# A hybrid streaming layer on one core: right-hand sums on VectorE alone, and output rows of two token blocks formed during the next block

## The chip, the core and the metric

The kernel runs on one core of one Trainium2 chip. The metric is the device time of one execution in microseconds, lower being better. Before the change it is 2352.13 us (median of 3 runs, 2347.12 to 2352.42). The engines are called as in the profile: PE (TensorE, the products), PEld (its weight loads), DVE (VectorE), ACT (ScalarE), POOL (GpSimd) and SP (SyncE, which issues the DMAs).

## What is computed

One layer of a streaming encoder over 2048 prompt tokens and 32 sample tokens of width 1024, all in float32: a norm, one input projection, attention and a state-space scan side by side, an output projection with a residual, and then a SwiGLU feed-forward network with a residual. The change lies in the last part alone:

```python
    h2 = _rmsnorm(x, lw['ln2_g']) * (1.0 + sc2) + sh2
    ff = (jax.nn.silu(h2 @ lw['w_gate']) * (h2 @ lw['w_up'])) @ lw['w_down']
    x = x + g2 * ff
```

`w_gate` and `w_up` are 1024 x 2816, `w_down` is 2816 x 1024.

## The kernel before

**Blocks and layers.** The feed-forward part begins at about 950 us of the span and runs to its end. It works on three token blocks one after the other (`PIECES`, `sb` = 0, 1, 2), of 704, 704 and 672 tokens. In each block there are four layers: `L.i` = 0 is gate and up (11 units `u`, each with a gate and an up half `m` = 0, 1), and `L.i` = 1, 2, 3 are thirds of the down projection (2 units each), whose results gather in the SBUF tiles `acc`. Features lie on the partitions, tokens in the free dimension, half a block (352 or 336 tokens) to a product.

**Seven products.** Each unit multiplies a left 2 x 2 arrangement (weights) with a right one (activations, the tiles `q00`, `q01`, `q10`, `q11`, in code `b11`, `b12`, `b21`, `b22`) by a scheme with seven products (`PRODUCTS`, steps p = 0 to 6) in place of eight. That needs sums of weight quarters on the left (`wr`, formed on POOL) and four sums of quarters on the right, once per layer, formed in `prepare_right` six steps ahead: t1 = b12 - b11, t3 = b22 - b12, t2 = b22 - t1 and t4 = b21 - t2, each written over one of its inputs (t1 and t2 over b11).

**Split operands.** A float32 product is made of three, of a high part and a rest on each side (`mm3`): ACT rounds the high part (`bh` for the right, `wh` for the left), DVE subtracts to get the rest (`bl`, `wl`). One step is thus 2 halves `m` x 4 x 3 = 24 products on PE, with results in the PSUM banks `fx`, `fy`, `fz`. After each step `finish` takes banks up: `c` tiles on ACT, DVE and POOL for gate and up, `acc` on DVE for down.

**Output rows.** When a unit `u` of the last down layer has done steps 5 and 6, `out_rows` begins for its half of the 1024 features: it loads residual rows `xr` through SP (6 buffers), then for each of 2 or 4 pieces of up to 128 tokens transposes four `acc` slices on PE into a PSUM bank (`fo`; the two banks of tag `ft` are shared with the transposes that build the next block's activations), adds the bank to `xr` on DVE, and stores the row through SP. A block has 12 such pieces. The generators stand in the list `live`, and each is moved on by one piece after every step.

**What sets the order.** The code gives a program order; a scheduler then places the instructions of each engine, and may pull an instruction forward as far as its inputs and free buffers allow. Each engine then runs its own list in order.

Of the kernel before, what the change touches and what calls it, by code (L numbers as in the profile page):

```python
# [16 lines left out]
MULT, ADD, SUB = ALU.mult, ALU.add, ALU.subtract  # L17
# [56 lines left out]
def hybrid_kernel(  # L74
# [10 lines left out]
    V, A, P, PE, SP = nc.vector, nc.scalar, nc.gpsimd, nc.tensor, nc.sync  # L85
    dbg = dbg or {}

    def tt(e, out, a, b, op):
        e.tensor_tensor(out, a, b, op=op)  # L89
# [10 lines left out]
    def act(out, a, func=AF.Copy, **kw):  # L100
        A.activation(out, a, func, **kw)  # L101
# [10 lines left out]
    def split(hi, lo, src, eh, el):  # L112
        cp(eh, hi, src)
        tt(el, lo, src, f(hi), SUB)
# [4 lines left out]
    def mm3(out, ah, al, bh, bl, start, stop, more=False):  # L119

        mm(out, ah, bh, start, False, more)
        mm(out, ah, bl, False, stop and al is None, more)
        if al is not None:
            mm(out, al, bh, False, stop, more)
# [83 lines left out]
    def advance(g, n=1):  # L208
        for _ in range(n):
            if next(g, None) is None:  # L210
                return
# [1226 lines left out]
    def h_steps(sb):  # L1438
        q = quads(4)
        qd[sb, 0] = q  # L1440
        w, col = HALF[sb], 0
        for grp in (PIECES[sb][0:3], PIECES[sb][3:6]):
            xs = []
            for j, r0, n in grp:
                m = 128 if j < NPT else DEC
                x = fp_["q"].tile([128, D], F32, tag="xf", name="xf", bufs=3)
                SP.dma_start(x[0:m], x1_d[j * 128:j * 128 + m])
                act(x[0:m], x[0:m], scale=r2[0:m, j:j + 1])
                xs.append((x, m, 0 if j < NPT else 1))
                yield 1  # L1450
            for k in range(KD):
                pb = fp_["t"].tile([128, 384], F32, tag="ft", name="ft")
                for i, (x, m, s) in enumerate(xs):
                    PE.transpose(pb[:, 128 * i:128 * i + m], x[0:m, k * 128:(k + 1) * 128], ident[0:m, 0:m])
                c = col
                o = grp[0][1]
                for s in range(2):
                    left = sum(n for j, _, n in grp if (j >= NPT) == s)
                    while left:
                        h, at = divmod(c, w)  # L1460
                        n = min(left, w - at)
                        act(q[k // 4][h][:, k % 4, at:at + n], pb[:, o:o + n], AF.Identity,
                            scale=sc2[:, k, s:s + 1], bias=sh2[:, k, s:s + 1])
                        c, o, left = c + n, o + n, left - n
                yield 1
            col = c
# [39 lines left out]
    def start_unit(n):  # L1506

        if n < len(steps) and steps[n][0].i == 0:
            L, u, _ = steps[n]
            raw[L, u] = [{t: quarter(L, u, m, t, wtile(4)) for t in ("21", "22", "11", "12")} for m in range(2)]  # L1510
            for r in raw[L, u]:
                r["s1"] = wtile(4)
                tt(P, r["s1"], r["21"], r["22"], ADD)
                tt(P, r["21"], r["11"], r["21"], SUB)
                r["s3"] = r["21"]
# [27 lines left out]
    def bparts(pool, slot, L):  # L1543
        return tuple(pool.tile([128, 4, HW], F32R, tag=f"b{t}{slot}", name=f"b{t}")[:, 0:L.kt, 0:L.w] for t in "hl")
# [55 lines left out]
    def prepare_right(n):  # L1600
        if n >= len(steps) or steps[n][1]:
            return
        L, _, p = steps[n]
        w = L.w
        (b11, b12), (b21, b22) = [[x[:, :, 0:w] for x in row] for row in qd[L.sb, L.i]]

        def parts(i, x):
            bn = PRODUCTS[i][1]
            h, l = bparts(fp_["v"] if i == 0 else pv, bn, L)
            split(h, l, x, A, V)  # L1610
            right[L, i] = (h, l)

        if p == 0:
            parts(0, b11)
            tt(V, b11, b12, b11, SUB)
            tt(P, b12, b22, b12, SUB)
        elif p == 1:
            parts(1, b21)
            parts(3, b11)
            tt(P, b11, b22, b11, SUB)  # L1620
            tt(V, b21, b21, b11, SUB)
        elif p != 3:
            parts(p, {2: b11, 4: b12, 5: b21, 6: b22}[p])
# [79 lines left out]

    def out_rows(L, half, pieces):

        hs_ = slice(half * 512, (half + 1) * 512)
        tiles = [acc[d] for d in range(4 * half, 4 * half + 4)]
        xs = []
        for j, r0, n in [PIECES[L.sb][i] for i in pieces]:
            xr = pwr.tile([128, 512], F32, tag="xr", name="xr", bufs=XR)[0:n]  # L1710
            SP.dma_start(xr, x1_d[j * 128 + r0:j * 128 + r0 + n, hs_])
            xs.append(xr)
        yield 1
        for i, xr in zip(pieces, xs):
            j, r0, n = PIECES[L.sb][i]
            col = sum(x[2] for x in PIECES[L.sb][:i])
            row = j * 128 + r0
            pb = fp_["t"].tile([128, 512], F32, tag="ft", name="fo")[0:n]
            for i in range(4):
                PE.transpose(pb[:, 128 * i:128 * i + 128], tiles[i][:, col:col + n], ident)  # L1720
            tt(V, xr, pb, xr, ADD)
            SP.dma_start((y_sample[0] if j >= NPT else y_prompt[0, row:row + n])[:, hs_], xr)
            yield 1

    live = []
    banks = {}
    cs, gs = {}, {}

    def keep():
        return pv.tile([128, HW], F32, tag="c", name="c", bufs=12)  # L1730
# [31 lines left out]
    def columns(L, j):  # L1762
        ns = L.w - DEC if L.sb == 2 and j else L.w
        return [(0, slice(0, ns))] + ([(1, slice(ns, L.w))] if ns < L.w else [])

    def finish(n):
        L, u, p = steps[n]
        w = L.w
        for m in range(2):
            x, y, z = (banks.get((t, m)) for t in "xyz")  # L1770
            if p in (0, 2, 4):
                c = keep()[:, 0:w]
                if L.i == 0:
                    act(c, x[:, 0:w])
                else:
                    i, j = {0: (0, 0), 2: (0, 1), 4: (1, 1)}[p]
                    d = 4 * u + 2 * m + i
                    for s, cols_ in columns(L, j):
                        act(c[:, cols_], x[:, cols_], scale=g2c[:, d, s:s + 1])
                cs[m, p] = c  # L1780
            if p in (1, 4, 5, 6):
                qd_ = {1: (0, 0), 4: (1, 1), 5: (1, 0), 6: (0, 1)}[p]
                bank = {1: z, 4: y, 5: x, 6: y}[p][:, 0:w]
                c = None if p == 5 else cs.pop((m, {1: 0, 4: 4, 6: 2}[p]))
                (finish_out if L.i else finish_in)(L, u, m, qd_, c, bank)
        if p > 4 and L.i == 3:
            live.append(out_rows(L, u, range(0, 2) if p == 5 else range(2, 6)))

    plain_right("21")
    for m, t in ((0, "21"), (0, "22")):  # L1790
# [26 lines left out]
    for n, (L, u, p) in enumerate(steps):  # L1817
        li = layers.index(L)
        if p == 0:
            start_unit(n + 7)  # L1820
        if L.i == 3 and u == 0 and p == 0 and L.sb < 2:
            coming.append(h_steps(L.sb + 1))
        if L.i == 0 and (u, p) == (5, 0) or L.i in (1, 2) and (u, p) == (0, 1):
            layers[li + 1].load()
        if L.i == 3 and u == 1 and p == 1:
            for _ in chain(*coming):
                pass
        if li == 0 and n > 3:
            advance(sums)
        elif li == 1 and (u, p) == (0, 0):  # L1830
            for _ in sums:
                pass
        load_left(n + FAR)
        prepare(n + AHEAD)
        prepare_right(n + 6)
        bh, bl = right[L, p]
        b = PRODUCTS[p][2]
        first = p in (0, 1, 3)
        for m in range(2):
            ah, al = left[n][m]  # L1840
            if first:
                banks[b, m] = fs1.tile([128, 512], F32, tag=f"{b}{m}", name=f"f{b}")
            dst = banks[b, m][:, 0:L.w]
            for k in range(L.kt):
                mm3(dst, ah[:, k], al[:, k], bh[:, k], bl[:, k], first and k == 0, k == L.kt - 1, not first)
        left.pop(n)
        finish(n)
        for g in chain(coming):
            advance(g, 4)
        for g in list(live):  # L1850
            if next(g, None) is None:
                live.remove(g)
# [53 lines left out]
```

## Time and profile before

| what | value |
|---|---|
| time, median of 3 runs | 2352.13 us (2347.12 to 2352.42) |
| the profiled execution, its own time | 2346.64 us |
| its span, first to last instruction | 2344.8 us |
| mean granted PE clock | 0.969 of full speed |
| DVE row sums `xr` | 36, 24.1 us in all |
| POOL right-hand sums (`q<-q,q`) | 23, 87.5 us in all |

The profile is one execution. A line of the timeline has the start and the length in us, engine, line of code, operation, the tile written and the tiles read, their shape and a count; in square brackets stands how long the engine was idle before it, and what ended that. `x` with a number counts instructions. Line 89 is the helper `tt` (a tensor-tensor operation), 98 is `stt`, 101 is `act`, 117 is `mm`; so groups are told apart by tiles.

### The profile page before, as it was taken

How to read it: one execution, taken by the hardware profiler on the slowest of the kernel's cores; microseconds unless marked ns; L12 is line 12 of the kernel's file. 1: busy time of each engine (PE TensorE's matmuls, PEld its weight loads, DVE VectorE, ACT ScalarE, POOL GpSimd, SP SyncE). 2: the span in 40 equal slices, each digit the busy share in tenths (PEclk: the TensorE clock that was granted, in tenths of full speed). 3: DMA queues.
4: the chain of work that ended last, by engine and by line, in shares of the span. 5: the costliest groups of instructions: out<-in, count | busy, mean ns of one | idle time of the engine just before them, and what ended most of it. 6: DMA issues, size and time to landing. Idle time of an engine off the chain costs nothing. (4 is left out here: it accounts for less than half of the span.)

```text
span 2344.8 us, 39041 instructions
## 1 busy us (share of the span) xinstructions
PE 2215.2 (94%) x13286; PEld 2055.6 (88%) x13286; DVE 1770.5 (76%) x2715; ACT 1258.6 (54%) x2544; POOL 1326.1 (57%) x1195
## 2 busy tenths in 40 slices
PE   7888998897899999999999998999999989999998
PEld 4577776786788888899999997999999989999998
DVE  6878875677877874867668889666588897777887
ACT  6655444456566655544345675444455744445663
POOL 1177775776466664678884246555522466655243
PEclk7899998998899999999999999999999999999999
DMA  7757676675422215567657545443365445433653
GB/s 232 261 168 238 193 218 213 205 237 173 110 73 88 76 53 179 153 200 222 199 178 220 167 137 177 146 138 98 105 200 168 127 146 155 132 107 119 193 162 120
DMA packets 429572, 380.12 MB, mean 162 GB/s; under 512 B 57326, under 2 KB 358986, under 8 KB 429372
## 3 DMA queue, kind: packets, MB, share of 16 engines
q1 hardware_dynamic: 429372, 377.63, 52.7%
q8 instruction: 104, 1.70, 0.3%
q14 instruction: 96, 0.79, 0.1%
HBM read 284.63 MB, written 92.91 MB: 161 GB/s over the span
## 5 line engine op out<-in xcount | busy, mean ns | idle before, releaser
L89 DVE TENSOR_TENSOR wl<-wr,wh 128x512 fp32r<-128x512 f32 (+1 forms) x708 | 717.5, 1031 | 223.1 <-ACT wh L101 218.2
L101 ACT ACTIVATE wh<-wr 128x512 fp32r<-128x512 f32 (+1 forms) x708 | 430.3, 616 | 529.7 <-PE fx L117 290.7
L117 PE MATMUL fx<-bh,wh 128*128 128x352 f32 (+1 forms) x1576 | 508.5, 323 | 9.5 <-DVE acc L98 5.5
L117 PE MATMUL fx<-bl,wh 128*128 128x352 f32 (+1 forms) x1576 | 506.6, 321 | 2.7 <-DVE bl L89 2.7
L117 PE MATMUL fx<-bh,wl 128*128 128x352 f32 (+1 forms) x1576 | 507.3, 322 | 0.0
L89 POOL TENSOR_TENSOR wr<-wr 128x512 f32<-128x512 f32 x256 | 379.8, 1493 | 197.6 <-DVE wl L89 148.0
L117 PEld LDWEIGHTS fx<-bh,wh 128*128 128x128 f32 x1576 | 298.4, 189 | 11.1 <-DVE acc L98 6.1
L117 PEld LDWEIGHTS fx<-bl,wh 128*128 128x128 f32 x1576 | 298.1, 189 | 3.7 <-DVE bl L89 3.7
L117 PEld LDWEIGHTS fx<-bh,wl 128*128 128x128 f32 x1576 | 297.6, 189 | 0.1
L117 PE MATMUL fy<-bh,wl 128*128 128x352 f32 (+1 forms) x792 | 254.0, 321 | 1.4 <-DVE wl L89 1.4
L117 PE MATMUL fy<-bh,wh 128*128 128x352 f32 (+1 forms) x792 | 254.6, 321 | 0.0
L117 PE MATMUL fy<-bl,wh 128*128 128x352 f32 (+1 forms) x792 | 253.9, 321 | 0.0
L89 POOL TENSOR_TENSOR c<-c 128x352 f32<-128x352 f32 (+1 forms) x96 | 139.2, 1451 | 132.9 <-ACT wh L101 89.9
L89 POOL TENSOR_TENSOR c<-c,acc 128x352 f32<-128x352 f32 (+1 forms) x72 | 84.7, 1180 | 173.1 <-ACT c L101 169.6
L89 POOL TENSOR_TENSOR q<-q,q 128x1408 f32<-128x1408 f32 (+3 forms) x23 | 87.5, 3809 | 121.1 <-DVE q L89 87.3
L89 DVE TENSOR_TENSOR bl<-q,bh 128x1408 fp32r<-128x1408 f32 (+3 forms) x85 | 150.2, 1770 | 5.5 <-ACT bh L101 5.5
L117 PEld LDWEIGHTS fy<-bh,wl 128*128 128x128 f32 x792 | 149.0, 188 | 1.7 <-DVE wl L89 1.7
L117 PEld LDWEIGHTS fy<-bh,wh 128*128 128x128 f32 x792 | 149.5, 189 | 0.0
L117 PEld LDWEIGHTS fy<-bl,wh 128*128 128x128 f32 x792 | 149.2, 188 | 0.0
L117 PE MATMUL fz<-bh,wl 128*128 128x352 f32 (+1 forms) x412 | 134.7, 327 | 8.1 <-DVE wl L89 8.1
L101 ACT ACTIVATE bh<-q 128x1408 fp32r<-128x1408 f32 (+3 forms) x85 | 108.9, 1286 | 52.5 <-DVE q L89 35.1
L117 PE MATMUL fz<-bl,wh 128*128 128x352 f32 (+1 forms) x412 | 133.6, 324 | 3.0 <-DVE bl L89 3.0
(388 smaller groups left out, 5235.4 us busy)
## 6 DMA issues: line engine op xcount, KB each, us to landing
wr<-in_w_gate_dram SPq DMA_DIRECT2D x132, 256.0 KB
wr<-in_w_up_dram SPq DMA_DIRECT2D x132, 256.0 KB
wr<-sd_d SPq DMA_DIRECT2D x96, 256.0 KB
wr<-in_w_down_dram SPq DMA_DIRECT2D x72, 256.0 KB
adw<-in_w_ada_dram SPq DMA_DIRECT2D x64, 256.0 KB
f_d<-c SPq DMA_DIRECT2D x88, 176.0 KB
sm<-sm_d SPq DMA_DIRECT2D x32, 448.0 KB
q<-f_d SPq DMA_DIRECT2D x16, 704.0 KB
```

What stands on the lines that cost most here:

```text
L89: e.tensor_tensor(out, a, b, op=op)
L101: A.activation(out, a, func, **kw)
L117: PE.matmul(out, lhsT, rhs, start=start, stop=stop, skip_group_check=more)
```

## The change

Two of the four right-hand sums in `prepare_right` go from POOL to DVE, where the other two are already. The generators of `out_rows` of blocks 0 and 1 are put on a list `held` in place of `live`; from the third gate-and-up unit of the next block on, after each step, the first of them moves on by one piece. Those of block 2 are driven as before.

```diff
         if p == 0:
             parts(0, b11)
             tt(V, b11, b12, b11, SUB)
-            tt(P, b12, b22, b12, SUB)
+            tt(V, b12, b22, b12, SUB)
         elif p == 1:
             parts(1, b21)
             parts(3, b11)
-            tt(P, b11, b22, b11, SUB)
+            tt(V, b11, b22, b11, SUB)
             tt(V, b21, b21, b11, SUB)
...
-    live = []
+    live, held = [], []
...
         if p > 4 and L.i == 3:
-            live.append(out_rows(L, u, range(0, 2) if p == 5 else range(2, 6)))
+            (live if L.sb == 2 else held).append(out_rows(L, u, range(0, 2) if p == 5 else range(2, 6)))
...
         for g in chain(coming):
             advance(g, 4)
+        if L.i == 0 and u > 1 and held and next(held[0], None) is None:
+            held.pop(0)
         for g in list(live):
             if next(g, None) is None:
                 live.remove(g)
```

The very first layer's sums, written apart at lines 1804 to 1811, are not touched; one of them stays on POOL.

What stands in the engines' lists then is the scheduler's. Up to about the end of the first block's gate-and-up layer the lists are the same. DVE at the start of the second block's gate-and-up layer, before the change (the tiles of this layer are `q00_15525` and its three neighbours; the names' numbers differ between the programs where tiles are new):

```order
L89 TENSOR_TENSOR bl_15978<-q00_15525,bh_15977 128x1408
L89 TENSOR_TENSOR wl_16126<-wr_15856,wh_16125 128x512
L89 TENSOR_TENSOR wl_16130<-wr_15864,wh_16129 128x512
L98 SCALAR_TENSOR_TENSOR acc_14653<-fy_16024,g2c_86,c_16001 128x352
L89 TENSOR_TENSOR bl_15974<-q10_15527,bh_15973 128x1408
L89 TENSOR_TENSOR xr_15805<-fo_15906,xr_15805 128x512
L89 TENSOR_TENSOR wl_16253<-wr_15852,wh_16252 128x512
L89 TENSOR_TENSOR xr_15844<-fo_15913,xr_15844 128x512
L98 SCALAR_TENSOR_TENSOR acc_14655<-fy_16034,g2c_86,c_16003 128x352
L89 TENSOR_TENSOR wl_16197<-wr_15868,wh_16196 128x512
L89 TENSOR_TENSOR q10_15527<-q10_15527,q00_15525 128x1408
L89 TENSOR_TENSOR bl_16096<-q01_15526,bh_16095 128x1408
```

The same place on DVE after the change, from the same `bl` on:

```order
L89 TENSOR_TENSOR bl_15938<-q00_15525,bh_15937 128x1408
L89 TENSOR_TENSOR wl_16068<-wr_15837,wh_16067 128x512
L89 TENSOR_TENSOR q01_15526<-q11_15528,q01_15526 128x1408
L89 TENSOR_TENSOR q00_15525<-q11_15528,q00_15525 128x1408
L89 TENSOR_TENSOR wl_16072<-wr_15845,wh_16071 128x512
L98 SCALAR_TENSOR_TENSOR acc_14653<-fy_15977,g2c_86,c_15961 128x352
L89 TENSOR_TENSOR bl_15934<-q10_15527,bh_15933 128x1408
L98 SCALAR_TENSOR_TENSOR acc_14655<-fy_15987,g2c_86,c_15963 128x352
L89 TENSOR_TENSOR wl_16166<-wr_15833,wh_16165 128x512
L89 TENSOR_TENSOR wl_16124<-wr_15849,wh_16123 128x512
L89 TENSOR_TENSOR xr_16741<-fo_16825,xr_16741 128x512
L89 TENSOR_TENSOR xr_16907<-fo_16953,xr_16907 128x512
```

Two sums, of `q01` and of `q00`, now stand in DVE's list, right behind the second `bl` of `q00`; the row sums `xr` are fewer and stand closer together. Behind these rows come, after the change,

```order
L89 TENSOR_TENSOR bl_16132<-q11_15528,bh_16131 128x1408
L89 TENSOR_TENSOR q10_15527<-q10_15527,q00_15525 128x1408
L89 TENSOR_TENSOR bl_16042<-q01_15526,bh_16041 128x1408
L89 TENSOR_TENSOR wl_16170<-wr_15841,wh_16169 128x512
L89 TENSOR_TENSOR c_16161<-fz_16173,c_16161 128x352
L89 TENSOR_TENSOR bl_15974<-q00_15525,bh_15973 128x1408
```

whose last row is the right part of product 2; before, it stood 19 rows behind the first `bl` shown, now 17. On PE, product 2 used to follow all 24 products of step 3 (`fy`) and 28 transposes since the first `fo` of this place; now it follows 14 and 20. Of the 12 row pieces, 8 stand within the first few steps of the layer, as the scheduler pulls them forward, and 4 in later steps.

DVE between the gate-and-up layer and the first down layer of block 0, as one piece of the difference (`-` before, `+` after; the `q` rows are the sums, and `q_12419` to `q_12422` are the four quarters `q00`, `q01`, `q10`, `q11`):

```order
 L89 TENSOR_TENSOR q_12419<-q_12420,q_12419 128x1408
 L89 TENSOR_TENSOR bl<-q_12421,bh 128x1408
-L89 TENSOR_TENSOR wl<-wr,wh 128x512 x5
+L89 TENSOR_TENSOR wl<-wr,wh 128x512 x2
+L89 TENSOR_TENSOR q_12420<-q_12422,q_12420 128x1408
+L89 TENSOR_TENSOR wl<-wr,wh 128x512 x3
 L89 TENSOR_TENSOR bl<-q_12419,bh 128x1408
 L89 TENSOR_TENSOR wl<-wr,wh 128x512
 L89 TENSOR_TENSOR c<-fy,c 128x352
 L89 TENSOR_TENSOR wl<-wr,wh 128x512
+L89 TENSOR_TENSOR q_12419<-q_12422,q_12419 128x1408
```

The sums are put between the same `wl` and `c` rows. At the start of the third block DVE has, after the change,

```order
L98 SCALAR_TENSOR_TENSOR acc_19930<-fx_21014,g2c_86,acc_19930 128x352
L98 SCALAR_TENSOR_TENSOR acc_19930<-fy_21128,g2c_86,c_21174 128x352
L89 TENSOR_TENSOR q01_20669<-q11_20671,q01_20669 128x4x336
L89 TENSOR_TENSOR q00_20668<-q11_20671,q00_20668 128x4x336
L89 TENSOR_TENSOR wl_21356<-wr_20986,wh_21355 128x512
L98 SCALAR_TENSOR_TENSOR acc_19934<-fy_21138,g2c_86,c_21178 128x352
L89 TENSOR_TENSOR wl_21219<-wr_20988,wh_21218 128x512
L98 SCALAR_TENSOR_TENSOR acc_19934<-fx_21024,g2c_86,acc_19934 128x352
L89 TENSOR_TENSOR xr_21890<-fo_21933,xr_21890 64x512
L89 TENSOR_TENSOR wl_21223<-wr_20996,wh_21222 128x512
L89 TENSOR_TENSOR xr_21892<-fo_21976,xr_21892 128x512
L89 TENSOR_TENSOR bl_21193<-q01_20669,bh_21192 128x4x336
```

The two sums are new there; before, the same rows stood without them, and by the `bl` of product 2 (`bl_21125`, three rows further: a sum, an `acc`, this `bl`) there were four `xr` where now there are two. The other row pieces of this block stand two by two in later steps.

## The prediction

> **What bounds the kernel now.** I read the busy times and the clock first, then the stretches (one row per stretch of the span, busy us and count of each engine), then TensorE's list of waits.
>
> ```profile
> span 2344.8 us, 39041 instructions
> PE 2215.2 (94%) x13286; PEld 2055.6 (88%) x13286; DVE 1770.5 (76%) x2715; ACT 1258.6 (54%) x2544; POOL 1326.1 (57%) x1195
> ...
> core 0: us, PE busy (x) PEld busy (x) DVE busy (x) ACT busy (x) POOL busy (x), PEclk, DMA share, GB/s
> 1240.00:1250.00 10.00, 9.32 (x59) 9.02 (x57) 10.00 (x9) 6.71 (x11) 5.53 (x2) 1.00 0.57 191
> 1250.00:1260.00 10.00, 7.76 (x39) 7.76 (x40) 10.00 (x9) 3.90 (x6) 5.78 (x2) 0.83 0.60 169
> 1410.00:1420.00 10.00, 6.11 (x24) 5.91 (x23) 10.00 (x10) 7.57 (x11) 10.00 (x6) 0.66 0.50 179
> 1880.00:1890.00 10.00, 6.51 (x33) 6.46 (x33) 9.35 (x10) 5.16 (x11) 8.90 (x7) 0.83 0.09 26
> 1410.00:1450.00 40.00, 29.61 (x174) 28.15 (x172) 40.00 (x38) 22.06 (x31) 25.07 (x13) 0.91 0.53 166
> 1450.00:1490.00 40.00, 39.94 (x256) 39.86 (x257) 27.45 (x38) 17.76 (x34) 24.05 (x17) 1.00 0.54 168
> 1500.00:1540.00 40.00, 40.00 (x253) 40.00 (x252) 23.07 (x31) 18.09 (x36) 21.77 (x16) 1.00 0.36 107
> 1880.00:1920.00 40.00, 32.44 (x194) 31.09 (x195) 39.35 (x38) 19.38 (x33) 26.96 (x16) 0.93 0.37 114
> 1960.00:2000.00 40.00, 40.00 (x261) 40.00 (x261) 32.74 (x33) 19.88 (x39) 25.84 (x19) 1.00 0.45 131
> ```
>
> TensorE is the bound, at 94%. In the middle of a block it never stops, and its pace is 40/253 = 0.158 us a product (352 columns), in the third block 40/261 = 0.153 (336 columns). At the start of the second block (1410 to 1450) and of the third (1880 to 1920) VectorE is the full engine, 40.00 and 39.35 of 40 us, and TensorE gets fewer products done. These two stretches, and three like them in small, are all that this change can give.
>
> Which waits they are (TensorE only, from 1195 us on), and how many of the products there are transposes of output rows, tile `fo`:
>
> ```profile
> PE fz L117 <- DVE wl L89: 8.1, 5, 4.0
> PE fx L117 <- DVE acc L98: 5.5, 2, 3.9
> PE fo L1720 <- DVE xr L89: 5.0, 6, 1.6
> PE fz L117 <- DVE bl L89: 3.0, 1, 3.0
> PE fx L117 <- DVE bl L89: 2.6, 2, 1.7
> PE fx L117 <- DVE c L89: 1.6, 2, 0.9
> ...
> 1410.00:1450.00 40.00, 4.84 (x34) 3.84 (x32) 5.40 (x8) 0.00 (x0) 0.91 0.53 166
> ...
> 1880.00:1920.00 40.00, 5.36 (x32) 3.76 (x32) 4.05 (x6) 0.00 (x0) 0.93 0.37 114
> ...
> 1409.61 0.60 PE L1720 MATMUL fo<-cpk,acc 128*128 128x128 f32 x4
> ```
>
> Every wait ends in VectorE. Four transposes in 0.60 us, the first ending 0.27 after its start, are 0.11 us each. **The loss at the second block's start**: 140 products x 0.158 + 34 x 0.11 = 25.9 of 40 us, so 14.1 lost. **At the third's**: 162 x 0.154 + 32 x 0.11 = 28.5, so 11.5 lost. Each begins with a long wait (3.9 us on `acc`, 4.0 on `wl`), after which the granted clock is low: 1410 to 1420 holds 20 + 4 products, 3.6 us of work, so 6.4 of the 14.1 us go with that wait; 1880 to 1890 holds 29 + 4, so 5.1 of the 11.5. Up to those two waits VectorE's order is what it was, and I leave them as they are. Open to the change are 7.7 and 6.4 us.
>
> **The sums, in price.** GpSimd has 23 of them, and VectorE runs the same shapes (min/median/max ns):
>
> ```profile
> L89 DVE TENSOR_TENSOR wl<-wr,wh x706: 541/694/3730, 953.6 to 2325.4; 128x512 fp32r<-128x512 f32 x157, 128x384 fp32r<-128x384 f32 x20
> ...
> L89 DVE TENSOR_TENSOR q<-q,q x25: 1196/1611/2706, 935.5 to 2289.2; 128x1408 f32<-128x1408 f32 x13, 128x1344 f32<-128x1344 f32 x6, 128x1056 f32<-128x1056 f32 x4, 128x1008 f32<-128x1008 f32 x2
> L89 POOL TENSOR_TENSOR q<-q,q x23: 2564/3574/5846, 955.9 to 2286.3; 128x1408 f32<-128x1408 f32 x11, 128x1344 f32<-128x1344 f32 x6, 128x1056 f32<-128x1056 f32 x4, 128x1008 f32<-128x1008 f32 x2
> ...
> 1416.78 8.26 POOL L89 TENSOR_TENSOR q<-q,q 128x1408 f32<-128x1408 f32 x2
> ...
> 1416.04 2.28 DVE L89 TENSOR_TENSOR bl<-q,bh 128x1408 fp32r<-128x1408 f32 x1
> 1418.24 7.36 DVE L89 TENSOR_TENSOR wl<-wr,wh 128x512 fp32r<-128x512 f32 x2
> 1425.52 0.57 DVE L98 SCALAR_TENSOR_TENSOR acc<-fy,g2c,c 128x352 f32<-128x352 f32 x1
> 1426.01 1.61 DVE L89 TENSOR_TENSOR bl<-q,bh 128x1408 fp32r<-128x1408 f32 x1
> 1427.55 0.68 DVE L89 TENSOR_TENSOR xr<-fo,xr 128x512 f32<-128x512 f32 x1
> 1428.15 0.67 DVE L89 TENSOR_TENSOR wl<-wr,wh 128x512 fp32r<-128x512 f32 x1
> ```
>
> 22 sums move (the first, written at L1805, stays). Beside two of them on GpSimd, VectorE's two `wl` took 7.36 us instead of 2 x 0.60 (0.60 from start to start, rows 1427.55 and 1428.15), and its `bl` 2.28 instead of 1.61: they cost VectorE 6.8 us while it was the bound. On VectorE itself the two take 2 x 1.54 (a `bl` of that shape takes 1426.01 to 1427.55). So 22 x 1.6 = 35 us more work for VectorE are less than what it now loses, where it is full: 3.7 us better for a pair. The unknown is whether a sum there meets other GpSimd work: 1.54 alone, 2.71 at worst (the group's maximum). I take 1.54 at the block starts: GpSimd then waited 12.99 us for VectorE,
>
> ```profile
> 1438.03 1.28 POOL L89 TENSOR_TENSOR wr<-wr 128x512 f32<-128x512 f32 x1 [12.99 <-DVE wl L89]
> ```
>
> so it has nothing else to run there; the worst case is kept for the range. The Trainium skill ("SBUF — State Buffer", section "Who interferes with whom") says that a VectorE instruction with both inputs in SBUF and a GpSimd one that reads SBUF exclude each other, the later waiting for the whole of the earlier. The 7.36 us beside 8.26 agree; were it simple sharing of bandwidth, the pair would still be about even and the first two terms below would be some 4 us smaller.
>
> **Second block's start.** TensorE's last long wait there (2.0 us before 1440.9) is for the third `bl` of the part `q00`, the right side of product 2, which is the first half of the row at 1438.31: it ended at 1439.9.
>
> ```profile
> 1433.51 0.51 DVE L89 TENSOR_TENSOR c<-fz,c 128x352 f32<-128x352 f32 x1
> ...
> 1438.31 4.76 DVE L89 TENSOR_TENSOR bl<-q,bh 128x1408 fp32r<-128x1408 f32 x2
> ```
>
> In the changed order, counted from the `bl` at 1416.04 (up to which nothing differs), the same `bl` stands behind 4 `bl` (that one and three more) and 3 sums at 1.54 us, 5 `wl` and 2 `xr` at 0.60, 2 `acc` at 0.49 (1425.52 to 1426.01) and a `c` at 0.5: 10.8 + 4.2 + 1.0 + 0.5 = 16.5 us. With its own 1.6 it ends at 1434.1, 5.8 us earlier. TensorE has then done less than before: 10 products of `fy` and 8 transposes come later, 1.6 + 0.9 us. That leaves 3.3, in which the wait of 3.0 on `bl` is contained. Of the waits of `fo` on `xr` behind this point I add 0.7: **4.0 us** of 7.7, between 0.5 (the three sums take 2.71 each, 3.5 us more) and 7.7. Eight of twelve row pieces still stand near this start: the scheduler pulls them forward; only four move to later steps.
>
> **Third block's start.**
>
> ```profile
> 1888.32 0.58 DVE L98 SCALAR_TENSOR_TENSOR acc<-fx,g2c,acc 128x352 f32<-128x352 f32 x1 [0.65 <-PE fx L117]
> ...
> 1905.33 1.54 DVE L89 TENSOR_TENSOR bl<-q,bh 128x1344 fp32r<-128x1344 f32 x1
> ```
>
> The `bl` of product 2 ended at 1906.87. In the new order it stands behind 5 `acc`, 3 sums, 1 `bl`, 3 `wl`, 2 `xr`: 2.5 + 4 x 1.47 + 5 x 0.60 = 11.4, plus its own 1.5 (1.47 from start to start, as 1344 columns to 1408): 1901.2, 5.7 us earlier, with 22 products and 8 transposes owed (3.4 + 0.9): 1.4. The row pieces here do spread, two to a step, so the waits of `fo` on `xr` (5.0 us over three starts) mostly go: I take 2.1. **3.5 us** of 6.4, between 0 and 6.4.
>
> **From gate and up to down.** In the first block TensorE lost 20 - 98 x 0.158 = 4.5 us between 1240 and 1260.
>
> ```profile
> 1242.37 1.61 DVE L89 TENSOR_TENSOR bl<-q,bh 128x1408 fp32r<-128x1408 f32 x1
> 1243.91 6.14 DVE L89 TENSOR_TENSOR wl<-wr,wh 128x512 fp32r<-128x512 f32 x5
> ```
>
> The five `wl` beside a sum took 6.14 instead of 3.0; now 3.0 plus a sum of 1.54, 1.5 us earlier, which halves the wait (2.9) and with it the slow clock: **2.5**, between 0 and 4.5. The same place in the other blocks has waits of 1.6 in all on `c` and some 1.2 on `wl`; `c` moves up in the order: **1.7** of 2.8. At the start of the last down layer 1.6 us on `acc`: **0.8**.
>
> **At nothing.** Transposes and row sums stay as many (12 pieces a block). The sums `xr` land where VectorE is busy 27.45 of 40 us; without that cover they cost 12 x 0.60 = 7.2 us a block. Row loads and stores move along SP's queue among weight loads:
>
> ```profile
> SPq L1711 <- DMA out_dram<-xr: 10.2, 6, 3.5
> ...
> POOL wr L89 <- DMA wr<-in_w_up_dram: 4.2, 1, 4.2
> ```
>
> From 1440 to 1560 SP stood 10.2 us behind row stores while GpSimd waited only once for weights and TensorE not at all: weights are asked for seven steps of 24 x 0.158 = 3.8 us ahead.
>
> **Sum.** 4.0 + 3.5 + 2.5 + 1.7 + 0.8 = 12.5 us. The profiled execution took 2346.64 us, so 2334.1. The runs shown have the median 2352.13, 5.5 us above it; as the time is a median, 2352.1 - 12.5 = **2339.6**.
>
> **Rivals.** *The waits only move* (0.24, with the forecast's lower tail within 0.3%): TensorE reaches product 2 sooner by the work it has put off, and waits there as long as it gained; what is left are the small places, 5.0 us: about 2347. For it: VectorE stays full in both stretches, since its list there shortens by about a tenth. Against it: TensorE has finished no less by 1450, as the put-off products must run anyway.
>
> *VectorE's list grows* (0.08): if freed GpSimd turns at once to weight sums `wr`, `wl` stays as slow as beside a sum, and the sums come on top. Twelve of the 22 stand where TensorE waits for VectorE (two at each of two block starts, three gate-to-down places and the last down layer): 12 x 1.6 = 19 us, less 10 `xr` x 0.60: 13 us slower, 2365. It decides if GpSimd stays as busy as the 25.07 us of 1410 to 1450 without its sums. The 12.99 us of waiting speak against it. The Trainium skill ("Perfetto Trace Analysis", section "Optimizing Scalar/DVE Operations") points that way, as it would take work off a saturated VectorE, to GpSimd too; it adds that the shared port may undo this, and the row of 7.36 us shows that it does.
>
> *The rows don't move* (0.12): the scheduler had put 8 of 12 at the second start anyway; if it is 12 in effect, only the sums pay: 12.5 - 2.1 - 0.6 = 9.8, 2342.
>
> **Chances.** The forecast has 0.56. Faster by over 0.3% (7.1 us, about what a measurement can tell from no change): 0.52 of the forecast (the rest of it ends under 7.1 us) and 0.10 of the third rival make 0.62; within 0.3%, with the first rival: 0.30; slower: 0.08. Range: all that is open, 7.7 + 6.4 + 4.5 + 2.8 + 1.6 = 23 us, gives 2329; the other end is no gain, 2352, which leaves out the second rival and little more.
>
> **What would show it.** Right: products in the 40 us from the first wait at each block start rise from 174 and 194 towards 200 and 220; one sum is left on GpSimd; the longest `wl` falls from 3730 ns towards 2000; the waits of 3.9 and 4.0 us are still there. Wrong: a new wait of `fx` on `bl` of 3 us or more at product 2, or a wait of TensorE on weights.

## The result and the profile after

| | median, us | range, us | runs |
|---|---|---|---|
| before | 2352.28 | 2347.12 to 2353.51 | 4 |
| after | 2331.42 | 2329.71 to 2334.11 | 4 |

The ratio after to before is **0.9928, 95% interval 0.9914 to 0.9942**: faster by 0.7%, some 17 us (0.0072 x 2352). The two profiled executions took 2346.64 us before and 2332.55 after; their spans, 2344.8 and 2330.8, are 14.0 us apart. But the lists are the same up to the end of the first block's gate-and-up layer, and there the changed kernel's execution was already behind: the first sum of `q` on GpSimd, which both kernels have, starts at 955.9 us before and at 960.3 after. So the two traces have to account for 4.4 + 14.0 = 18.4 us from there on.

The page of the changed kernel (busy time and share of each engine), and the stretches that answer to those of before. The first long wait at the second block's start ends 0.9 us earlier in this trace than before (1413.19 for 1414.10), the one at the third block's 6.6 us earlier (1876.85 for 1883.49), so their stretches of 40 us are shifted by as much. The 20 us from 1244.30 answer to those from 1240 before, as TensorE is 4.3 us behind there.

```profile
span 2330.8 us, 39040 instructions
PE 2211.3 (95%) x13286; PEld 2055.1 (88%) x13286; DVE 1718.3 (74%) x2737; ACT 1261.2 (54%) x2544; POOL 1256.3 (54%) x1173
...
1409.10:1449.10 40.00, 32.90 (x194) 31.72 (x193) 40.00 (x44) 24.01 (x35) 21.57 (x13) 0.91 0.51 164
1873.40:1913.40 40.00, 34.91 (x210) 34.20 (x211) 36.97 (x43) 20.35 (x35) 26.31 (x14) 0.91 0.29 90
1244.30:1264.30 20.00, 20.00 (x126) 19.80 (x125) 20.00 (x20) 13.04 (x21) 6.03 (x3) 1.00 0.62 184
```

VectorE has 22 instructions more (2737 to 2715) and is busy 52 us less (1718.3 to 1770.5). In the two stretches TensorE does 194 and 210 products where it did 174 and 194; VectorE is still full in the first. In the 20 us between gate and up and down it does 126 products where there were 59 + 39 = 98, at the full clock (1.00).

How many of those products are transposes of output rows (the same stretches, tile `fo` alone), and TensorE's list of waits from 1190 us on, after the change:

```profile
1409.10:1449.10 40.00, 4.38 (x31) 3.36 (x29) 5.33 (x8) 0.00 (x0) 0.91 0.51 164
1873.40:1913.40 40.00, 3.27 (x24) 2.81 (x24) 4.04 (x6) 0.00 (x0) 0.91 0.29 90
...
PE fz L117 <- DVE wl L89: 4.0, 1, 4.0
PE fx L117 <- DVE acc L98: 3.8, 1, 3.8
PE fx L117 <- DVE bl L89: 3.7, 2, 2.9
PE fo L1721 <- DVE xr L89: 1.4, 2, 1.2
PE fy L117 <- DVE acc L98: 0.8, 1, 0.8
```

Two waits are as before: 4.0 us on `wl` and 3.8 on `acc`. Gone are four others of `fz` on `wl`, the 1.4 us of `fy` on `wl`, those of `fx` on `c`, `fz` on `bl`, and most of `fo` on `xr`. One has come: 2.9 us of `fx` on `bl`.

The groups that answer to `wl` and `q` of before (min/median/max ns):

```profile
L89 DVE TENSOR_TENSOR wl<-wr,wh x708: 542/692/1795, 931.4 to 2311.3; 128x512 fp32r<-128x512 f32 x155, 128x384 fp32r<-128x384 f32 x22
...
L89 DVE TENSOR_TENSOR q<-q,q x47: 1193/1608/2705, 939.9 to 2276.5; 128x1408 f32<-128x1408 f32 x23, 128x1344 f32<-128x1344 f32 x12, 128x1056 f32<-128x1056 f32 x8, 128x1008 f32<-128x1008 f32 x4
L89 POOL TENSOR_TENSOR q<-q,q x1: 4541/4541/4541, 960.3 to 960.3; 128x1408 f32<-128x1408 f32 x1
```

The longest `wl` is 1795 ns where it was 3730; its median is the same (692 to 694). The sums on VectorE last what they lasted there before.

The second block's start after the change, from the timelines of TensorE, VectorE and GpSimd:

```profile
1413.19 0.66 PE L117 MATMUL fx<-bh,wh 128*128 128x352 f32 x1 [3.81 <-DVE acc L98]
...
1415.13 2.28 DVE L89 TENSOR_TENSOR bl<-q,bh 128x1408 fp32r<-128x1408 f32 x1
1417.33 0.68 DVE L89 TENSOR_TENSOR wl<-wr,wh 128x512 fp32r<-128x512 f32 x1
1417.93 3.15 DVE L89 TENSOR_TENSOR q<-q,q 128x1408 f32<-128x1408 f32 x2
1421.01 0.68 DVE L89 TENSOR_TENSOR wl<-wr,wh 128x512 fp32r<-128x512 f32 x1
...
1432.17 1.61 DVE L89 TENSOR_TENSOR bl<-q,bh 128x1408 fp32r<-128x1408 f32 x1
...
1433.83 0.43 PE L117 MATMUL fx<-bl,wh 128*128 128x352 f32 x1 [2.86 <-DVE bl L89]
...
1434.36 2.47 POOL L89 TENSOR_TENSOR c<-c 128x352 f32<-128x352 f32 x1 [18.43 <-DMA wr<-in_w_up_dram]
```

Where two `wl` took 7.36 us beside GpSimd's pair of sums, there are now a `wl` of 0.68, both sums in 3.15, and a `wl` of 0.68. GpSimd stands idle 18.43 us; the row puts the end of that down to a load of weights, but none of TensorE's waits is for weights. The last `bl` shown is the right part of product 2, and TensorE waits 2.86 us for it.

### The profile page after: what moved, and what is told of

Same layout as the page of the kernel before. It is cut to its first block, busy times and chain, and to the rows that moved or that the text cites. A ratio compares the mean times of both kernels' runs of the same rounds, so it can differ in the third digit from the quotient of the medians.

```text
span 2330.8 us, 39040 instructions
## 1 busy us (share of the span) xinstructions
PE 2211.3 (95%) x13286; PEld 2055.1 (88%) x13286; DVE 1718.3 (74%) x2737; ACT 1261.2 (54%) x2544; POOL 1256.3 (54%) x1173
## 4 chain that ended last, share of the span: by engine, by line
PE 63%; DVE 6%; ACT 2%; issue 2%; POOL 1%; DMA 1%; SPq 0%; DVEq 0%; POOLq 0%; ACTq 0%
PE fx L117 30%; PE fy L117 15%; PE fz L117 8%; PE co L117 5%; PE cb L117 1%; PE ob L117 1%; DVE wl L89 1%; PE pt L1070 1%; PE ft L1454 1%; ACT pbuf L101 1%; DVE ss L1332 1%; DVE bl L89 0%; PE fo L1721 0%; PE s L117 0%; DVE gl L89 0%
## 5 line engine op out<-in xcount | busy, mean ns | idle before, releaser
L89 DVE TENSOR_TENSOR wl<-wr,wh 128x512 fp32r<-128x512 f32 (+1 forms) x708 | 641.0, 921 | 252.2 <-ACT wh L101 248.9
L89 POOL TENSOR_TENSOR wr<-wr 128x512 f32<-128x512 f32 x256 | 388.0, 1525 | 185.6 <-DVE wl L89 138.9
L89 POOL TENSOR_TENSOR c<-c,acc 128x352 f32<-128x352 f32 (+1 forms) x72 | 93.0, 1296 | 311.0 <-ACT c L101 293.2
L89 DVE TENSOR_TENSOR bl<-q,bh 128x1408 fp32r<-128x1408 f32 (+3 forms) x85 | 140.7, 1660 | 5.1 <-ACT bh L101 5.1
L117 PE MATMUL fz<-bh,wh 128*128 128x352 f32 (+1 forms) x412 | 133.6, 325 | 1.0 <-ACT wh L101 0.9
```

The source lines that it names most:

```text
L117: PE.matmul(out, lhsT, rhs, start=start, stop=stop, skip_group_check=more)
```

## The experiments

Ten kernels. The first four share one set of 17 runs of the kernel before (median 2350.87 us), the next four one of 10 (2349.98), the last two one of 11 (2349.32). My theory: GpSimd's sums cost because VectorE stands still beside them, and the rows add a little. The rival: the sums matter only through the time at which their own results are ready.

### One part of the change alone

The sums alone (output rows as before):

```diff
-            tt(P, b12, b22, b12, SUB)
+            tt(V, b12, b22, b12, SUB)
...
-            tt(P, b11, b22, b11, SUB)
+            tt(V, b11, b22, b11, SUB)
```

> The kernel before with the two GpSimd sums put on VectorE, and the output rows driven as before. Theory S (the sums carry the gain, since a sum on GpSimd shuts VectorE's subtractions out for its whole length, and takes longer itself): 11 to 16 us faster than before, the waits between gate-and-up and down layers (2.9 us near 1249, 0.6 to 0.9 near 1722, 1733, 2182 and 2192) gone, at the block starts some waits of the row transposes on VectorE left. Theory R (the spread of the output rows carries it): 0 to 5 us faster, since VectorE gets 35 us more work.

2330.38 us (2326.86 to 2335.73), ratio 0.9909 [0.9889, 0.9929]: 20.5 us, more than the 11 to 16 of theory S.

The rows alone (the sums stay on GpSimd):

```diff
-            live.append(out_rows(L, u, range(0, 2) if p == 5 else range(2, 6)))
+            (live if L.sb == 2 else held).append(out_rows(L, u, range(0, 2) if p == 5 else range(2, 6)))
...
+        if L.i == 0 and u > 1 and held and next(held[0], None) is None:
+            held.pop(0)
```

> The kernel before with its sums on GpSimd as they were, and only the output rows of blocks 0 and 1 driven beside the next block's products. Theory S: 0 to 4 us faster, the waits of the row transposes on VectorE (5.0 us in all before) fall to about 1.4, the waits between gate-and-up and down layers stay. Theory R: 8 to 15 us faster.

2350.64 us (2344.14 to 2356.16), ratio 1.0000 [0.9988, 1.0013]. So the sums carry the whole gain and the rows, as far as this can tell (0.13%, 3 us), none. TensorE's waits in that run, and its second block's start:

```profile
PE fz L117 <- DVE wl L89: 10.3, 6, 4.6
...
PE fy L117 <- DVE wl L89: 3.1, 2, 2.3
...
PE fo L1721 <- DVE xr L89: 2.6, 4, 1.2
...
1414.35 8.23 POOL L89 TENSOR_TENSOR q<-q,q 128x1408 f32<-128x1408 f32 x2
...
1415.79 7.34 DVE L89 TENSOR_TENSOR wl<-wr,wh 128x512 fp32r<-128x512 f32 x2
```

The held rows do take the waits of `fo` on `xr` from 5.0 to 2.6 us; but the two `wl` stand 7.34 us beside the two sums as they did, and the waits on `wl` rise from 8.1 and 1.4 (`fz` and `fy`) to 10.3 and 3.1 us. Of that rise 1.7 us lie at 1249.39, where the lists are still those of before, so the rows have no part in it. Behind that place the waits just moved: this trace is 2.4 us ahead of before's at the second block's first long wait (it ends at 1411.65 for 1414.10), 0.8 at the third's (1882.69 for 1883.49) and again 2.4 at the end (spans 2342.4 and 2344.8).

One sum alone (the first of the two lines above; the second stays on GpSimd):

> The kernel before with only b22 - b12 on VectorE; b22 - t1 stays on GpSimd, and the rows are driven as before. If each sum on GpSimd costs by itself (exclusion of VectorE), about half of what both sums give, 5 to 8 us faster; between gate-and-up and down the wait near 1249 shrinks, since this is the sum that runs beside the five wl there, while the one wl of 3.2 us behind it stays. If what counts is only the chain that ends in product 2 (the sum left on GpSimd feeds it), 0 to 3 us.

2339.20 us (2335.92 to 2346.05), ratio 0.9951 [0.9932, 0.9971]: 11.7 us, about half of what both give (more than the 5 to 8 expected), so each costs by itself.

### Does VectorE stand still, or is the sum's result late?

All four sums are on VectorE here, the rows as before, and GpSimd has idle work behind each moved sum: in the one kernel it reads the two quarters again and writes a tile that nobody reads, in the other it reads one column and then fills that tile three times. Both have 4 residual-row buffers in place of 6, for room.

```diff
+    def idle(L, x, y):
+        t = pv.tile([128, 4, 288], F32, tag="idle", name="idle")
+        tt(P, t[:, 0:L.kt], x[:, :, 0:288], y[:, :, 0:288], SUB)
...
             tt(V, b12, b22, b12, SUB)
+            idle(L, b22, b12)
...
             tt(V, b11, b22, b11, SUB)
+            idle(L, b22, b11)
```

> All four sums on VectorE, output rows driven as before the change. In addition GpSimd subtracts the same two quarters behind each moved sum (128 x 1152 elements of float32) into a tile that nobody reads; this is idle work, and to make room for it the residual rows have 4 buffers in place of 6. Theory 1 (a sum on GpSimd costs because VectorE's own instructions stand still while GpSimd reads SBUF): VectorE's wl beside these idle sums last 3 us and more again, and of the 20.5 us that the two sums alone gained (2350.9 to 2330.4) at least 5 go back: 2336 to 2350. Theory 2 (only the time until the sum itself is ready counts, since the steps behind it wait for its result; nobody waits for the idle one): 2328 to 2333, the longest wl under 2000 ns.

In the second kernel the body is instead

```diff
-        tt(P, t[:, 0:L.kt], x[:, :, 0:288], y[:, :, 0:288], SUB)
+        tt(P, t[:, 0, 0:1], x[:, 0, 0:1], y[:, 0, 0:1], SUB)
+        for _ in range(3):
+            P.memset(t[:, 0:L.kt], 0.0)
```

> The control to the idle sums: the same places, the same 4 buffers, but GpSimd subtracts one column and then fills the idle tile three times with zeros, so that it is busy without reading SBUF. Theory 1 (reading excludes): the longest wl stays under 2000 ns and the time is that of the two sums alone, 2330 plus or minus 3. If being busy is enough (GpSimd's weight sums come later, or writes exclude as well): as the idle sums, 2336 to 2350. Theory 2: 2328 to 2333.

And without idle work, but with the 4 buffers:

> All four sums on VectorE, rows driven as before the change, no idle work, and 4 residual-row buffers in place of 6: the two runs with idle work without the idle work. If the 10 us that the run with the memsets lost against the two sums alone came of the buffers (its waits of fo on xr rose from 3.2 to 6.4 us): 2337 to 2342. If they came of GpSimd being busy (its weight sums come later): 2329 to 2333.

| | median, us | ratio, 95% interval |
|---|---|---|
| idle sums | 2361.34 (2359.41 to 2365.44) | 1.0052 [1.0040, 1.0065] |
| idle fills | 2340.71 (2339.10 to 2342.78) | 0.9961 [0.9948, 0.9975] |
| neither, 4 buffers | 2335.80 (2329.65 to 2339.84) | 0.9939 [0.9922, 0.9956] |

Of the kernel with idle sums, and then of the one with fills: VectorE's and GpSimd's busy times, GpSimd's idle work by group, and VectorE's `wl` (min/median/max ns).

```profile
PE 2219.8 (94%) x13286; PEld 2056.9 (87%) x13286; DVE 1792.8 (76%) x2737; ACT 1260.8 (53%) x2544; POOL 1315.5 (56%) x1195
...
L89 POOL TENSOR_TENSOR idle<-q,q x22: 2054/3064/5757, 1249.5 to 2302.8; 128x1152 f32<-128x1152 f32 x16, 128x864 f32<-128x864 f32 x6
...
L89 DVE TENSOR_TENSOR wl<-wr,wh x708: 542/693/3175, 929.4 to 2339.5; 128x512 fp32r<-128x512 f32 x155, 128x384 fp32r<-128x384 f32 x22
```

```profile
PE 2213.6 (95%) x13286; PEld 2057.5 (88%) x13286; DVE 1728.9 (74%) x2737; ACT 1260.2 (54%) x2544; POOL 1360.9 (58%) x1261
...
L1604 POOL MEMSET idle<- x66: 819/1063/1075, 1256.5 to 2284.5; 128x1152 f32 x48, 128x864 f32 x18
...
L89 DVE TENSOR_TENSOR wl<-wr,wh x708: 540/693/1800, 933.3 to 2317.7; 128x512 fp32r<-128x512 f32 x155, 128x384 fp32r<-128x384 f32 x22
```

VectorE has the same 2737 instructions in both, and in neither trace does an engine wait for the idle work. Beside sums the longest `wl` is 3175 ns, beside fills 1800, and VectorE is busy 64 us longer (2.9 for each of 22, about the 3.06 that one lasts); GpSimd is the less busy of the two there. The time is 20.6 us longer, which is as much as the moved sums had gained (20.5). The rival, that only the sum's own result counts, is out: it forecast 2328 to 2333. Theory 1 had the direction and the `wl` right, but 2361 lies above its 2336 to 2350 too: it counted only what the move had gained, but here VectorE runs the sums itself and stands still beside the idle ones as well (busy 1792.8 us, 1770.5 before the change). This is the rule of the Trainium skill, "SBUF — State Buffer", section "Who interferes with whom", in both halves: a VectorE instruction with two SBUF inputs contends with a GpSimd one that reads SBUF, and not with one that only writes it.

My own expectation for the fills was 2330 plus or minus 3 and missed. Some 5 us of the 10 go with the 4 buffers (0.9939 to 0.9909; the intervals overlap a little), less than the first and more than the second of the two expectations. The trace of that kernel shows where most of them go: at the very end, VectorE waits for a residual row to be loaded,

```profile
2329.36 0.69 DVE L89 TENSOR_TENSOR xr<-fo,xr 128x512 f32<-128x512 f32 x1 [4.14 <-DMA xr<-x_d]
```

as the load could start only when a store had freed one of the 4 buffers (in the chain that ended last stand a store of 2.05 us and then this load, 3.96 us). With 6 buffers (the sums alone) the last four row sums follow one another without a stop. The idle sums and the fills have the same wait (3.81 and 3.79 us), so it does not touch the comparison of the two. Of the rest, if there is one (0.9961 to 0.9939, overlapping too), the traces show that the fills have 4.7 us of `fo` on `xr` at the third block's start, where the 4 buffers alone have 1.0; why stays open.

### Where the gain is made

The sums on VectorE only at the starts of the second and third block (4 of 22):

```diff
-            tt(P, b12, b22, b12, SUB)
+            tt(V if L.i == 0 else P, b12, b22, b12, SUB)
...
-            tt(P, b11, b22, b11, SUB)
+            tt(V if L.i == 0 else P, b11, b22, b11, SUB)
```

> Of the 22 sums only the four at the start of the gate-and-up layers of the second and third block go to VectorE; the rows as before the change. Theory (the gain is made at the places, and the two block starts give 3.4 to 3.9 and 2.9 us of it): 2344.4, ratio 0.997, with more products in the two stretches of 40 us (some 195 and 210) and 98 products between 1240 and 1260 as before. Rival (each sum moved gives the same, 20 us / 22): 2347.2, ratio 0.9985. If the block starts were most of it: 2338 or less.

2343.59 us (2338.83 to 2348.72), ratio 0.9974 [0.9961, 0.9987]. The three places in this run, the stretches shifted by what TensorE is ahead of before's there (3.1, 2.9 and 5.0 us):

```profile
1236.90:1256.90 20.00, 16.51 (x94) 16.21 (x93) 20.00 (x16) 11.06 (x18) 11.87 (x5) 0.91 0.62 182
1407.10:1447.10 40.00, 32.48 (x193) 31.40 (x192) 40.00 (x44) 23.51 (x35) 19.28 (x13) 0.91 0.55 173
1875.00:1915.00 40.00, 34.58 (x208) 33.67 (x209) 38.34 (x42) 20.43 (x35) 24.84 (x14) 0.91 0.33 100
```

The block starts fill up as in the changed kernel (193 and 208 products, 174 and 194 before), the place between gate and up and down does not (94, and 98 before). The block starts thus give 6.1 us (0.0026 x 2350), and the larger part of the 0.0091 that the sums alone give is made at the other places. That each sum gives the same share is not excluded: its 0.9985 lies in the interval.

### Can the two waits that are left go?

Ahead of both, GpSimd has additions of the down layers (`c <- c, acc`, L1755) between its weight sums. These 72 additions moved to VectorE as well, on top of the change:

```diff
-            tt(P, c, c, o, ADD)
+            tt(V, c, c, o, ADD)
```

> The changed kernel with the 72 additions of acc to c in the down layers (GpSimd, 0.9 to 2.3 us each) on VectorE as well. By exclusion (an operation that GpSimd takes away from VectorE costs VectorE about as long as it would take itself): the first waits at the block starts (3.8 and 4.0 us, with the low clock behind them) shrink, 3 to 8 us faster than the changed kernel. By load (VectorE is full where these additions stand, and gets 72 x 0.5 = 36 us more): no faster, or up to 10 us slower than the changed kernel.

2331.48 us (2327.46 to 2334.65), ratio 0.9913 [0.9896, 0.9931]: no faster than the changed kernel, as the expectation by load had it. The same with the rows as before the change:

> Both sums on VectorE and also the 72 additions of the down layers' c tiles (L1755), with the rows driven as before the change. In the run with the additions on VectorE and the rows held, a wait of fo on xr of 4.5 us near 1433 gave back what the shorter waits at the block starts had gained. If that wait came of the rows standing close together there, it is gone here, and the time is 3 to 6 us under the changed kernel: 2325 to 2328. If VectorE's fuller list at the block start makes it, whatever the order of the rows: 2330 to 2333.

2330.14 us (2329.08 to 2330.52), ratio 0.9916 [0.9902, 0.9929]. Its waits begin with

```profile
PE fo L1720 <- DVE xr L89: 6.3, 5, 4.6
PE fx L117 <- DVE acc L98: 2.2, 1, 2.2
```

The wait of 4.0 us on `wl` is gone, and one of 4.6 on `xr` has come at the second block's start; as it comes with held and with unheld rows, the rows do not make it, and my theory of it fell. The additions in the second block alone, with both sums on VectorE and the rows as before:

```diff
-            tt(P, c, c, o, ADD)
+            tt(V if L.sb == 1 else P, c, c, o, ADD)
```

> Both sums on VectorE, rows as before the change, and the additions of the down layers' c tiles on VectorE in the second block alone (24 of 72). With all 72 there the waits at the start of the third block fell from 4.4 us to under 1 and a wait of fo on xr of 4.6 us came at the start of the second. If the two belong to the additions of the block that ends there, only the gain is left: 2325 to 2327. If the lists of both places hang together: 2329 to 2333.

**2324.81 us (2321.69 to 2328.99), ratio 0.9893 [0.9876, 0.9910]**: faster than both kernels, its interval wholly under that of the changed kernel (0.9914 to 0.9942). With that of the sums alone (0.9889 to 0.9929), on which it is built, the interval overlaps, so the time does not show clear of noise what the additions add. All its waits, and its third block's start (TensorE gets there 8.4 us earlier than before):

```profile
PE fo L1720 <- DVE xr L89: 3.8, 4, 1.9
PE fx L117 <- DVE acc L98: 3.2, 1, 3.2
PE fx L117 <- DVE bl L89: 3.0, 2, 2.1
PE fy L117 <- DVE acc L98: 1.3, 1, 1.3
...
1871.60:1911.60 40.00, 37.26 (x247) 35.84 (x246) 40.00 (x48) 20.19 (x35) 29.17 (x14) 1.00 0.44 139
```

No wait on `wl` is left, none of 3.3 us or more, and in that stretch TensorE does 247 products (194 before) at a clock of 1.00. By these waits the additions pay at the end of the second block and not at that of the first.

## Why the prediction was right, and where it was not

The forecast was 2339.6, faster; the time is 2331.4, inside the range but near its fast end (2329). The gain was undersized: 12.5 us would be a ratio of 0.9947, just outside the measured interval. The mechanism held: a sum on GpSimd costs VectorE more than a sum on VectorE, since VectorE's own instructions stand still beside it. Of its terms:

- **The pair's price, right.** A sum on VectorE took 1.57 there (3.15 for two) where 1.54 was taken, and the `wl` beside it went back to 0.68. From the `bl` at its head to the end of product 2's `bl` lie 18.65 us (1415.13 to 1433.78) where 16.5 + 1.6 = 18.1 were counted.
- **Second block's start, nearly right.** 163 products and 31 transposes are 163 x 0.158 + 31 x 0.11 = 29.2 of 40 us, so 10.8 lost where it was 14.1: 3.3 us for a forecast of 4.0. (The wait for product 2 before, which the forecast put at 2.0 us, is 1.75 in TensorE's row.)
- **Third block's start, a little less.** 186 x 0.154 + 24 x 0.11 = 31.3, so 8.7 lost where it was 11.5: 2.8 for 3.5. The two sums were counted at 1.47 each, and took 4.31 us together, beside additions and a weight sum that GpSimd still had there:

```profile
1880.44 2.30 POOL L89 TENSOR_TENSOR c<-c,acc 128x352 f32<-128x352 f32 x2
1882.71 2.61 POOL L89 TENSOR_TENSOR wr<-wr 128x512 f32<-128x512 f32 x1
...
1882.43 4.31 DVE L89 TENSOR_TENSOR q<-q,q 128x1344 f32<-128x1344 f32 x2
```

- **From gate and up to down, the term that was mis-sized.** "1.5 us earlier, which halves the wait (2.9)" gave 2.5; the whole 4.4 came (98 to 126 products at 0.158), and with the small waits of the other blocks (2.8 for 1.7) and of the last down layer (1.6 for 0.8) 8.8 us for a forecast of 5.0. None of these waits is in the list after. Here is the place before, VectorE's and TensorE's rows, then after:

```profile
1251.50 0.68 DVE L89 TENSOR_TENSOR wl<-wr,wh 128x512 fp32r<-128x512 f32 x1
...
1252.24 0.66 PE L117 MATMUL fz<-bh,wl 128*128 128x352 f32 x1 [2.92 <-DVE wl L89]
```

```profile
1247.38 1.61 DVE L89 TENSOR_TENSOR bl<-q,bh 128x1408 fp32r<-128x1408 f32 x1
1248.92 1.28 DVE L89 TENSOR_TENSOR wl<-wr,wh 128x512 fp32r<-128x512 f32 x2
1250.12 1.61 DVE L89 TENSOR_TENSOR q<-q,q 128x1408 f32<-128x1408 f32 x1
1251.66 1.88 DVE L89 TENSOR_TENSOR wl<-wr,wh 128x512 fp32r<-128x512 f32 x3
1253.47 1.61 DVE L89 TENSOR_TENSOR bl<-q,bh 128x1408 fp32r<-128x1408 f32 x1
1255.00 0.68 DVE L89 TENSOR_TENSOR wl<-wr,wh 128x512 fp32r<-128x512 f32 x1
```

  From the head `bl` to the end of the `wl` that TensorE waited for lay 9.8 us before (1242.37 to 1252.18); now 8.3 (1247.38 to 1255.68). The 1.5 us were counted right. What the forecast did not look at is TensorE's own list. Before, the product that needs this `wl` (1252.24) comes right behind the one at 1248.99. In the changed kernel the scheduler has put 14 other products between the same two, 2 of `fz` and 12 of `fx`:

```profile
1253.26 0.32 PE L117 MATMUL fx<-bh,wl 128*128 128x352 f32 x1
...
1255.73 0.43 PE L117 MATMUL fz<-bh,wl 128*128 128x352 f32 x1
```

  They cover 14 x 0.158 = 2.2 us; with the 1.5 that is 3.7, more than the wait of 2.9. How long the wait is depends besides on how far VectorE is behind TensorE when they meet, and that differs between executions. The kernel with the rows alone has before's lists up to here, and waited 4.6 us:

```profile
1249.39 0.66 PE L117 MATMUL fz<-bh,wl 128*128 128x352 f32 x1 [4.63 <-DVE wl L89]
```

  There TensorE is 4.55 us earlier than before (the product ahead of the wait starts at 1244.44 for 1248.99), the head `bl` only 2.84 (1239.53 for 1242.37), and the difference of 1.7 us is what the wait has grown by. With both sums on VectorE the same wait was none in the changed kernel and in that with 4 buffers, 0.6 us with the sums alone and 1.3 beside the idle fills; beside the idle sums it was 2.6. Why VectorE is further behind in one execution than in another stays open.
- **The rows, wrong.** 2.1 + 0.7 us of the sum were theirs. The rows alone give 1.0000 [0.9988, 1.0013]. The third rival (only the sums pay) was right on this, but not in its reason, that the rows stay where they were: they did move, and took 2.4 us of waits of `fo` on `xr` away without any gain. Its time, 2342, was made of the other terms and too long (and took 0.6 us off for the 0.7 of the second start).
- **The first rival's wait came.** `fx` waits on `bl` at product 2 for 2.86 us. It stands in place of before's 3.0 on `bl`, 1.7 on `bl` and 1.4 on `wl` there, so it did not take back the gain.
- **Left as they are** were the waits of 3.9 and 4.0, and they are (3.8 and 4.0). The last experiment shows that the one on `wl` goes with GpSimd's additions ahead of it.

The sum by places is 3.3 + 2.8 + 4.4 + 2.8 + 1.6 = 14.9. That is near the 14.0 us between the spans, but only by chance, as the changed kernel's execution began 4.4 us behind: from the first sum of `q` on the traces hold 18.4 us, of which 5.3 lie ahead of the first long wait at the second block's start, 5.7 between that and the third block's, and 7.4 behind it. So the places, as counted, leave 3.5 us unexplained. Of the forecast's terms those of the two block starts were too large (7.5 for 6.1), those of the small places too small (5.0 for 8.8); that they partly cancel is luck.

## What to carry to other kernels

Before work is left on GpSimd because VectorE is full, look in the timeline at what VectorE's instructions with two SBUF inputs take beside it: here 22 sums, 83 us on GpSimd, made VectorE 52 us busier than running them itself. When sizing such a removal, a wait at a meeting point of two engines is not a stock to subtract from. Compare the lists of both engines there: the shorter list of VectorE gave 1.5 us, 14 products put ahead in TensorE's another 2.2. And two executions of one list had waits of 2.9 and 4.6 us there, so let the range reach to the whole wait and the slow clock behind it. Before closing a sum against two traces, look how far apart they are ahead of the change (4.4 us here). And what a move saves at one block's end (the additions in the second block) can be given back at another, so try it place by place.

## What was not expected of the hardware

GpSimd filling an SBUF tile cost VectorE's instructions nothing that can be seen: 66 fills of about 1.06 us, and VectorE busy 1728.9 us, where the same kernel without them (4 buffers) had 1736.2 and the sums alone 1732.3. And executions drift apart ahead of the change by as much as a term of the forecast: at the first sum of `q`, with the same lists up to there, the profiled one of before is at 955.9 us, that with the rows alone at 951.8, and that of the changed kernel at 960.3.
